# Two-block transformer layer, one core: the loop over further expert tiles stands ahead of the last step's products

## The chip, the core and the metric

The kernel runs on one core of one Trainium2 chip. The metric is device time in microseconds (us) of one execution. Engines are named as in the profile: PE (matrix products; PEld is its weight load), DVE, ACT, POOL and SP; SP only issues transfers and waits.

## What is computed

Two layers follow each other on 512 tokens of 1024 features in float32. The first has a gated short convolution, sparse attention and a dense feed-forward part. The second has latent attention, a convolution branch, and a mixture of 32 experts of which each token takes two; a last normalization ends it. All that this change touches lies in the mixture:

```python
a = jnp.einsum('td,edf->tef', t, e_gate[gi])
u = jnp.einsum('td,edf->tef', t, e_up[gi])
hid = jax.nn.silu(a) * u * combine[:, gi, :, None]
out = out + jnp.einsum('tef,efd->td', hid, e_down[gi])
...
x = x + gt2 * hierarchical_moe(...)
return rmsnorm(x, final_norm_g)
```

## The kernel before

The mixture works on tiles of tokens that were sorted by expert. Sixteen paired tiles hold up to 64 tokens of one expert and 48 of another. What does not fit goes into further tiles of 64 tokens of one expert. How many of these there are is known only at run time. The first further tile is always worked, as the last of 17 steps (step 16, group 16 in `seq`); the others are worked by `loop()` (L1679), a loop in hardware registers from 1 to a count read from the tile `ei` (L1683). In the profiled execution the count is 1, so the body is not run; what is run is the test of the loop and what stands at its exit.

A step i has these parts, each issued in program order (`keep`):

- `weights(i)` (L1640): the experts' weights come in thirds of 512 KB, each one transfer on SP's queue (L1293). A paired step takes six, step 16 takes three, by `further(0)` (L1629). Their buffers are a ring.
- `hidden(i)` (L1595): products of features and weights on PE (L1592), three of eight blocks first; then `turn(i - 1)` (L1702), which transposes the hidden rows of the step before on PE (L1609) and copies them out on DVE into `ht` (L1611); then the other five blocks; then the activation on ACT (L1603) and DVE (L1604) into `hs`.
- `rows_in_place(i + 1)` (L1697): transposed features of the next step's rows, in the tile `xtb`.
- `finish(i - 1)` (L1705): second products of the step before (`down`, L1620 on PE, L1621 on DVE into `y`). Up to step 14 an indirect transfer issued by POOL then adds the rows to the table `acc` in DRAM (L1625, "the add"). For steps 15 and 16 `keep_on_chip` (L1666) splits `y` into two parts (ACT L306, DVE L307) and makes a selection matrix `oh` (DVE L1670).

With LOOP = 16 the loop is issued at the end of step 16's turn in the Python loop: behind step 16's products and behind `finish(15)`, and in front of `turn(16)` and `finish(16)`. At the start of step 15 the program issues the weights of step 16 and after them the load of the last norm's gain (`gfin`: 512 KB into a row buffer, L1721). After the loop the table `acc` is loaded again in four transfers (`fin`, L1741, two on SP, two on ACT), PE adds the rows kept on chip by products with `oh` (L1751), and the last norm and the stores follow.

Before the loop's exit every engine waits, in a row of pair-wise semaphore waits, for every other engine and for every transfer queue: each engine's part of this is booked on L1684. The tiles `xwe`, `xtb` and the two `y` are in a pool of four buffers of 512 KB (`x_tile`, L466).

Of the kernel before, what the change touches and what calls it, by code (L numbers as in the profile page):

```python
# [72 lines left out]
GA1 = (0, 0, 0, 1, 0, 1, 0, 1, 1, 0)  # L73
NW = 9
NCH = 2
LOOP = 16
LF = True
NX = 18
NR = 8
# [157 lines left out]
def build(tc, A, out, taps=None):  # L237
# [35 lines left out]
    def psum(tag, name=None):  # L273
        return psp.tile([P, S], F32, tag=tag, bufs={"mm": 3, "lg": 2, "tp": 2, "po": 1}[tag],
                        name="p" + (name or tag))
# [167 lines left out]
    class Ssq:  # L443
# [4 lines left out]
        def add(self, t, scale=1.0, pin=False):  # L448
            sq = blk("sq" if self.acc else "acc")
            i = act(sq, t, ACT.Square, scale=scale)  # L450
            if pin:
                keep(i)
            if self.acc is None:
                self.acc = sq
            else:
                self.eng.tensor_tensor(self.acc, self.acc, sq, ALU.add)
# [9 lines left out]
    def x_tile(name):  # L466
        return xpool.tile([P, D], F32, tag="x", bufs=4, name=name)
# [14 lines left out]
    xg = []  # L482
# [412 lines left out]
    xg = []  # L895
    s1, s2 = Ssq(G), Ssq(G)
    r = None
    for half in range(2):
        hid = []
        st = {}  # L900
# [399 lines left out]
    def more(n, after=False):  # L1300
        for _ in range(n):
            e, j = THIRDS[len(we)]
            we[e, j] = load(A["we"][order[e]], j, after)
# [242 lines left out]
    def rows_of(ws):  # L1546
        return PR if len(ws) == 2 else 64
# [3 lines left out]
    def gather(xg, si_, n):  # L1551

        rows_in.append(keep(nc.gpsimd.indirect_dma_start(  # L1553
            out=xg[:n], out_offset=None, in_=htok,
            in_offset=bass.IndirectOffsetOnAxis(ap=si_[:n], axis=0), bounds_check=S - 1, oob_is_err=False)))
        return xg
# [4 lines left out]
    xtb = x_tile("xt")  # L1561
    yb = [x_tile("y%d" % i) for i in range(2)]
    ohb = ml[0].tile([P, S], F32R, name="oh")

    def scaled(n, xg, st):

        for q in range(2):
            o = slice(q * S, (q + 1) * S)
            keep(act(xg[:n, o], xg[:n, o], ACT.Copy, scale=st[:n, 2:3]))

    def features(n, xg, xt):

        xt = xt.rearrange("p (k t) -> p k t", k=DB)
        for q in range(2):
            pt = psum("tp")
            for j in range(4):
                k, o = 4 * q + j, slice(j * P, j * P + n)
                keep(nc.tensor.transpose(pt[:, o], xg[:n, k * P:(k + 1) * P], ident[:n, :n]))
            for j in range(4):
                k, o = 4 * q + j, slice(j * P, j * P + n)  # L1580
                if j % 2:
                    keep(act(xt[:, k, :n], pt[:, o], ACT.Identity, scale=gs2[:, k:k + 1],  # L1582
                             bias=adac[:, 24 + k:25 + k]))
                else:
                    keep(TS(xt[:, k, :n], pt[:, o], gs2[:, k:k + 1], adac[:, 24 + k:25 + k], ALU.mult, ALU.add))
        return xt

    def products(pg, ws, xt, ks):
        n = rows_of(ws)
        for k in ks:  # L1590
            for j, w in enumerate(ws):
                keep(mm(pg[64 * j:min(64 * j + 64, n), :256], xt[:, k, 64 * j:min(64 * j + 64, n)],  # L1592
                        w[k // 4][:, k % 4 * 256:(k % 4 + 1) * 256], start=(k == 0), stop=(k == DB - 1)))

    def hidden(ws, xt, st, between=None):  # L1595
        n = rows_of(ws)
        pg = psum("lg")
        products(pg, ws, xt, range(3))
        if between:
            between()  # L1600
        products(pg, ws, xt, range(3, DB))
        hs = mr[0].tile([P, 2, P], F32, tag="hs", bufs=2, name="hs")
        keep(act(hs[:n, 0], pg[:n, 0:128], ACT.Silu))  # L1603
        keep(STT(hs[:n, 1], pg[:n, 128:256], st[:n, 1:2], hs[:n, 0], ALU.mult, ALU.mult))  # L1604
        return hs

    def turned(n, hs):
        pt = psum("tp")
        keep(nc.tensor.transpose(pt[:, :n], hs[:n, 1], ident[:n, :n]))  # L1609
        ht = mr[0].tile([P, P], F32, tag="ht", bufs=2, name="ht")  # L1610
        keep(V.tensor_copy(ht[:, :n], pt[:, :n]))  # L1611
        return ht

    def down(ws, ht, y):
        n = rows_of(ws)
        for q in range(2):
            py = psum("mm")
            for j, w in enumerate(ws):
                o = slice(64 * j, min(64 * j + 64, n))
                keep(mm(py[o], ht[:, o], w[2][:, q * S:(q + 1) * S]))  # L1620
            keep(TT(y[:n, q * S:(q + 1) * S], py[:n], gt2r[:n, q * S:(q + 1) * S], ALU.mult))  # L1621
# [7 lines left out]
    def further(t):  # L1629

        ev = nc.sync.value_load(ei[0:1, bass.ds(t, 1)], min_val=0, max_val=31)
        src = A["we"][bass.ds(ev, 1)].rearrange("o p n -> p (o n)")
        return [[load(src, j) for j in range(3)]]
# [6 lines left out]
    def weights(i, after=True):  # L1640
        g = seq[i]
        if g == 16:
            wes[i] = further(0)
            return
        more(upto[g] - len(we), after)
        wes[i] = [[we[n, j] for j in range(3)] for n in (2 * g, 2 * g + 1)]
# [32 lines left out]
    def loop():  # L1679
        for j in range(LOOP + 1, 17):  # L1680
            weights(j, LF)

        ntl = nc.values_load(ei[0:1, 16:17], min_val=1, max_val=16)  # L1683
        with tc.For_i(1, ntl) as t:  # L1684
            st = mr[0].tile([P, 4], F32, name="lsl")[:, :3]

            nc.sync.dma_start(slots[16 * P:].rearrange("(g p) c -> p g c", p=P), slt[:, 16:])
            nc.sync.dma_start(st[:64], slots[bass.ds(16 * P + 64 * t, 64)])
            ix = mr[0].tile([P, 1], I32, name="lix")
            V.tensor_copy(ix[:64], st[:64, 0:1])  # L1690
            w = further(t)
            xg = gather(xgb[0], ix, 64)
            scaled(64, xg, st)
            down(w, turned(64, hidden(w, features(64, xg, xtb), st)), yb[0])
            add(64, yb[0], ix, acc)

    def rows_in_place(i):  # L1697
# [7 lines left out]
    def finish(i):  # L1705
        if i < 17 - NCH:
            down(wes.pop(i), hts.pop(i), yb[i % 2])
            add(size(i), yb[i % 2], sidx[:, seq[i]:seq[i] + 1], acc if seq[i] == 16 else halves[seq[i] // 8])
        else:
            keep_on_chip(i)  # L1710
# [4 lines left out]
    for i in range(17):  # L1715
        if i not in wes:
            weights(i)
        if i == 15:
            weights(16)
            gfr = xgb[i % NQ]  # L1720
            keep(nc.sync.dma_start(gfr, A["gfin"].broadcast_to([P, D])))  # L1721
        hss[i] = hidden(wes[i], xts.pop(i), slt[:, seq[i]], (lambda: turn(i - 1)) if i else None)
        if i < 16:
            rows_in_place(i + 1)
        if i < 15:
            scaled(size(i + 2), xgb[(i + 2) % NQ], slt[:, seq[i + 2]])
        if i:
            finish(i - 1)
        if i == LOOP:
            loop()  # L1730
    turn(16)
    finish(16)

    if LOOP == 17:
        loop()
# [70 lines left out]
```

## Time and profile before

| | us |
|---|---|
| median of three runs | 1369.53 (1366.01 to 1370.35) |
| the profiled execution | 1369.21 |
| its span, first to last instruction | 1367.4 |

The profile page gives busy times, the span in 40 slices, and the granted clock of PE in tenths of full speed. The timeline lists instructions of an engine in order: start and duration in us, line, operation, output and inputs, count, and in brackets the idle time ahead of it with what ended it. An entry "L1684" stands for the loop's test and exit on some engine. The list of windows gives each engine's busy time in a stretch, the granted clock, the busy share of the 16 transfer engines and the rate. PE's fp32 products count twice in the trace: one product in the program is two records.

### The profile page before, as it was taken

What the parts mean: (1) busy time and instruction counts of PE and PEld (TensorE: products, weight loads), DVE (VectorE), ACT (ScalarE), POOL (GpSimd) and SP (SyncE); (2) the same over time, 40 slices, a digit from 0 to 9 for tenths busy, and PEclk for the clock granted to TensorE, in tenths of its full rate; (3) what the DMA queues carried; (4) which work ended last, traced back from release to release, by engine and by line L of the source; (5) the groups of instructions that cost most, each with busy time, mean ns of one, the idle gap of its engine ahead of it and who ended that gap; (6) DMA issues with size and microseconds to landing.
All of it is one profiled execution on the core that took longest, in us unless ns stands there. A gap on an engine that the chain in (4) does not pass through costs nothing. (4 is left out here: it accounts for less than half of the span.)

```text
span 1367.4 us, 16340 instructions
## 1 busy us (share of the span) xinstructions
PE 1263.3 (92%) x5800; PEld 948.5 (69%) x5800; DVE 834.5 (61%) x1459; ACT 544.5 (40%) x898; POOL 643.8 (47%) x365
## 2 busy tenths in 40 slices
PE   6798999999999999999999988999979999689875
PEld 4576887777888878777788767778846587445432
DVE  5857785543758643367246577989977762644324
ACT  4433335666433332122324344243376542155322
POOL 4514447554646554444747645256734372123311
PEclk9999999999999999999999999899989999789997
DMA  5214323233245644565323223233330169989883
GB/s 166 71 51 152 103 91 139 87 107 123 93 138 186 203 164 142 190 246 197 112 85 103 71 93 93 73 120 132 116 108 24 48 245 367 339 290 277 264 298 124
DMA packets 69538, 206.02 MB, mean 151 GB/s; under 512 B 9539, under 2 KB 14331, under 8 KB 69456
## 3 DMA queue, kind: packets, MB, share of 16 engines
q1 hardware_dynamic: 60608, 190.67, 41.0%
q0 software_dynamic: 4048, 8.01, 2.5%
q10 hardware_dynamic: 4800, 6.29, 1.3%
q8 instruction: 46, 0.75, 0.2%
q14 instruction: 36, 0.29, 0.1%
HBM read 191.90 MB, written 21.61 MB: 156 GB/s over the span
## 5 line engine op out<-in xcount | busy, mean ns | idle before, releaser
L337 POOL TENSOR_TENSOR wl<-raw,wh 128x1024 fp32r<-128x1024 f32 (+2 forms) x180 | 420.2, 2337 | 440.4 <-ACT wh L336 336.1
L336 ACT ACTIVATE wh<-raw 128x1024 fp32r<-128x1024 f32 (+2 forms) x183 | 183.3, 1004 | 348.7 <-DMA raw<-in_w_dn 71.6
L345 PE MATMUL pw_gu<-xg,wh 128*128 128x512 f32 x704 | 168.6, 391 | 0.0
L345 PEld LDWEIGHTS pw_gu<-xg,wh 128*128 128x128 f32 x704 | 131.5, 188 | 31.3 <-issue 3.4
L701 DVE SCALAR_TENSOR_TENSOR ad<-raw,cact,ad 128x512 f32<-128x512 f32 x84 | 91.2, 1133 | 44.9 <-DMA raw<-in_ada 44.9
L345 PE MATMUL pw_cv<-h,wh 128*128 128x512 f32 x320 | 83.8, 416 | 8.9 <-ACT wh L336 6.2
L345 PE MATMUL pw_gu<-xg,wl 128*128 128x512 f32 x352 | 87.9, 390 | 0.0
L1039 DVE SCALAR_TENSOR_TENSOR ptaps<-u,vec,ptaps 128x511 f32<-128x511 f32 (+28 forms) x116 | 85.7, 739 | 3.3
L345 PE MATMUL pw_dn<-h,wh 128*128 128x512 f32 x352 | 85.5, 390 | 0.0
L1592 PE MATMUL plg<-we,xt 128*64 128x256 f32 (+1 forms) x528 | 74.4, 400 | 10.6 <-DMA we<-in_we 6.9
L345 PEld LDWEIGHTS pw_cv<-h,wh 128*128 128x128 f32 x320 | 63.9, 202 | 23.8 <-ACT wh L336 7.5
L345 PEld LDWEIGHTS pw_dn<-h,wh 128*128 128x128 f32 x352 | 65.9, 188 | 14.5 <-issue 0.8
L345 PEld LDWEIGHTS pw_gu<-xg,wl 128*128 128x128 f32 x352 | 65.8, 188 | 13.7
L1592 PEld LDWEIGHTS plg<-we,xt 128*64 128x64 f32 (+1 forms) x528 | 40.2, 135 | 42.0 <-issue 13.1
L345 PE MATMUL pw_gb<-h,wh 128*128 128x512 f32 x256 | 64.3, 394 | 0.0
L345 PE MATMUL pw_ga<-h,wh 128*128 128x512 f32 x256 | 62.3, 391 | 0.0
L345 PEld LDWEIGHTS pw_ga<-h,wh 128*128 128x128 f32 x256 | 47.7, 188 | 10.3 <-issue 0.8
L345 PEld LDWEIGHTS pw_gb<-h,wh 128*128 128x128 f32 x256 | 47.4, 188 | 9.2
L729 DVE TENSOR_SCALAR e<-e,ri 128x512 f32<-128x512 f32 (+2 forms) x64 | 48.2, 755 | 1.5
L1553 POOL DMA_INDIRECT xg<-htok,sidx x17 | 17.4, 1025 | 67.3 <-ACT xt L1582 43.9
L727 ACT ACTIVATE e<-e,mx 128x512 f32<-128x512 f32 (+2 forms) x64 | 40.8, 638 | 20.3 <-DVE mx L770 13.2
L907 POOL TENSOR_TENSOR t<-t,m 128x512 f32<-128x512 f32 x22 | 32.7, 1488 | 30.0 <-ACT t L906 30.0
(461 smaller groups left out, 2490.9 us busy)
## 6 DMA issues: line engine op xcount, KB each, us to landing
we<-in_we SPq DMA_DIRECT2D x99, 512.0 KB, 9.7
raw<-in_ada SPq DMA_DIRECT2D x48, 512.0 KB, 3.8
raw<-in_w_gu SPq DMA_DIRECT2D x44, 512.0 KB, 4.3
raw<-in_w_cv SPq DMA_DIRECT2D x20, 512.0 KB, 3.5
raw<-in_w_ga SPq DMA_DIRECT2D x16, 512.0 KB, 3.6
raw<-in_w_gb SPq DMA_DIRECT2D x16, 512.0 KB, 3.4
raw<-in_w_o SPq DMA_DIRECT2D x16, 512.0 KB, 3.5
spill<-g SPq DMA_DIRECT2D x24, 256.0 KB, 2.3
```

The lines of the kernel that those rows point to most:

```text
L336: act(wh[:, :n], raw[:, :n], ACT.Copy)
L337: (eng or G).tensor_tensor(wl[:, :n], raw[:, :n], f(wh[:, :n]), ALU.subtract)
L345: mm(ps, w[:, o + k * M:o + (k + 1) * M], xs[k][i], start=(first and j == 0), stop=(last and j == n - 1))
L701: STT(t, raw[:, o], cact[:, k:k + 1], t, ALU.mult, ALU.add)
L727: act(e, e, ACT.Exp, scale=-1.0, bias=mx[:, h_, b:b + 1], accum_out=sm[:, h_, b:b + 1])
L729: (G if b in NP else V).tensor_scalar(e, e, r, None, ALU.mult)
L907: G.tensor_tensor(t, t, r, ALU.mult)
L1039: keep(STT((a if k else y)[:, s:], u[:, :S - s], w, a[:, s:], ALU.mult, ALU.add))
L1553: rows_in.append(keep(nc.gpsimd.indirect_dma_start(out=xg[:n], out_offset=None, in_=htok, in_offset=bass.IndirectOffsetOnAxis(ap=si_[:n], ...
L1592: keep(mm(pg[64 * j:min(64 * j + 64, n), :256], xt[:, k, 64 * j:min(64 * j + 64, n)], w[k // 4][:, k % 4 * 256:(k % 4 + 1) * 256], start=( ...
```

## The change

LOOP is 15 in place of 16. So `loop()` is issued at the end of step 15's turn: behind `finish(14)`, and in front of step 16's products, `turn(15)`, `finish(15)`, `turn(16)` and `finish(16)`. The loop's body gets a feature tile of its own, `lxt`, since `xtb` now holds step 16's features while the loop stands. It is a fifth tile of the pool of four and takes the buffer of `xwe`. The line at the head of `loop()` that issues the weights of the steps from LOOP + 1 to 16 was empty before; it now issues `weights(16)` once more, after step 15 had already done so, and step 16 uses the second set.

```diff
-LOOP = 16
+LOOP = 15
...
     def loop():
         for j in range(LOOP + 1, 17):
             weights(j, LF)
+        lxt = x_tile("lxt")
 
         ntl = nc.values_load(ei[0:1, 16:17], min_val=1, max_val=16)
...
-            down(w, turned(64, hidden(w, features(64, xg, xtb), st)), yb[0])
+            down(w, turned(64, hidden(w, features(64, xg, lxt), st)), yb[0])
```

On PE before, from step 16's products to its second products (the rows between the two L1684 groups are the loop's body, which is not run; `plg` are hidden products, `ptp` transposed tiles, `pmm` second products):

```order
L1592 MATMUL plg<-we,xt 64x256 x3
L1609 MATMUL ptp<-cst,hs 128x112
L1592 MATMUL plg<-we,xt 64x256 x5
L1620 MATMUL pmm<-we,ht 64x512
...
L1684 COMPARE_AND_BRANCH
L1684 UNCONDITIONAL_BRANCH x2
...
L1609 MATMUL ptp<-cst,hs 128x64
L1620 MATMUL pmm<-we,ht 64x512 x2
```

On PE now, the same stretch:

```order
L1685 COMPARE_AND_BRANCH
L1685 UNCONDITIONAL_BRANCH x2
...
L1592 MATMUL plg<-we,xt 64x256 x3
L1609 MATMUL ptp<-cst,hs 128x112
L1592 MATMUL plg<-we,xt 64x256 x5
L1620 MATMUL pmm<-we,ht 64x512
...
L1609 MATMUL ptp<-cst,hs 128x64
L1620 MATMUL pmm<-we,ht 64x512 x2
```

The exit moved from between the second products of step 15 and the transposition of step 16 to ahead of step 16's first products.

On SP, as a piece of the difference, at the end of the weights (`gfin` is the gain):

```order
 L1293 DMA we<-in_we 128x1024
-L1721 DMA xg_9270<-in_gfin 128x1024
-L1684 COMPARE_AND_BRANCH
...
+L1293 ISA
+L1293 DMA we<-in_we 128x1024
+L1293 ISA
+L1293 DMA we<-in_we 128x1024
+L1293 ISA
+L1293 DMA we<-in_we 128x1024
+L1722 DMA xg_9270<-in_gfin 128x1024
+L1685 COMPARE_AND_BRANCH
```

Three more loads of 512 KB stand ahead of the gain's load and of the loop's test.

## Rows read from the trace of the kernel before

**Rows 1.** The page: span, and the granted clock of PE in 40 slices.
```profile
span 1367.4 us, 16340 instructions
PEclk9999999999999999999999999899989999789997
```
**Rows 2.** Timeline of PE, end of step 15 to the kept rows: start, duration, line.
```profile
1322.97 2.51 PE L1620 MATMUL pmm<-we,ht 128*64 128x512 f32 x8
1329.04 2.68 PE L1592 MATMUL plg<-we,xt 128*64 128x256 f32 x6 [3.56 <-SPq L1684]
...
1334.49 1.88 PE L1620 MATMUL pmm<-we,ht 128*64 128x512 f32 x7
1338.99 0.27 PE L1609 MATMUL ptp<-cst,hs 64*128 64x64 f32 x1 [2.63 <-DVEq L1684]
1340.49 3.67 PE L1620 MATMUL pmm<-we,ht 128*64 128x512 f32 x4 [1.22 <-DVE ht L1611]
1344.09 0.80 PE L1751 MATMUL ppo<-yh,oh 112*128 112x512 f32 x1
```
**Rows 3.** Waits of SP, 1310 to 1368 us: total, times, longest.
```profile
SPq L1684 <- DMA acc<-y,sidx: 5.5, 1, 5.5
SPq L1684 <- DVEq L1683: 2.7, 1, 2.7
```
**Rows 4.** The loop's lines by engine: duration ns min/median/max, first and last start.
```profile
L1683 POOLq TENSOR_LOAD <-ei x1: 496/496/496, 1326.6 to 1326.6; - x1
...
L1683 DVEq TENSOR_LOAD <-ei x1: 544/544/544, 1337.2 to 1337.2; - x1
...
L1684 PEldq EVENT_SEMAPHORE  x13: 51/51/364, 1336.4 to 1338.6; - x13
...
L1684 DVEq EVENT_SEMAPHORE  x13: 21/50/50, 1338.5 to 1339.9; - x13
```
**Rows 5.** Timeline of POOL, the last add; and L1625's times to landing, three adds.
```profile
1326.84 1.45 POOL L1625 DMA_INDIRECT acc<-y,sidx  x1 [8.02 <-DVE y L1621]
...
DMA to landing us min/median/max: 8.0/8.5/8.6
```
**Rows 6.** Windows: busy us per engine (PE, PEld, DVE, ACT, POOL), clock, transfer share, GB/s.
```profile
1300.00:1326.00 26.00, 21.59 (x128) 10.16 (x127) 8.78 (x23) 8.19 (x19) 3.90 (x3) 1.00 0.97 331
1328.00:1332.00 4.00, 2.96 (x7) 1.28 (x7) 0.00 (x0) 0.00 (x0) 0.29 (x1) 0.65 0.59 134
1332.00:1335.00 3.00, 3.00 (x16) 1.84 (x17) 0.28 (x2) 0.27 (x1) 0.00 (x0) 0.90 0.05 12
1341.00:1344.00 3.00, 3.00 (x4) 0.46 (x2) 0.85 (x3) 0.63 (x1) 0.00 (x0) 0.50 1.00 388
1339.40:1346.00 6.60, 5.51 (x9) 2.27 (x10) 2.94 (x6) 1.26 (x2) 0.00 (x0) 0.50 0.84 318
```
**Rows 7.** Timeline of SP: the last five weight loads, and the gain's.
```profile
1316.85 3.14 SPq L1293 DMA_DIRECT2D we<-in_we  x5
1320.52 0.34 SPq L1721 DMA_DIRECT2D xg<-in_gfin  x1
```
**Rows 8.** Timeline of DVE, between the second products of steps 15 and 16.
```profile
1335.59 1.52 DVE L1621 TENSOR_TENSOR y<-pmm,gt2r 112x512 f32<-112x512 f32 x2 [0.25 <-PE pmm L1620]
1337.03 0.68 DVE L307 TENSOR_TENSOR yl<-y,yh 112x512 fp32r<-112x512 f32 x1
1337.63 0.86 DVE L1670 TENSOR_SCALAR oh<-moeb,slt 64x128 fp32r<-64x128 bf16 x4
1340.21 0.22 DVE L1611 COPY ht<-ptp 128x64 f32<-128x64 f32 x1 [1.72 <-PE ptp L1609]
1340.35 0.68 DVE L307 TENSOR_TENSOR yl<-y,yh 112x512 fp32r<-112x512 f32 x1
```
**Rows 9.** Timeline of PE earlier: two runs of 14 products behind idle time.
```profile
1287.74 3.23 PE L1592 MATMUL plg<-we,xt 128*48 128x256 f32 x14 [2.57 <-DMA we<-in_we]
...
1299.87 1.93 PE L1592 MATMUL plg<-we,xt 128*48 128x256 f32 x14 [1.36 <-DMA we<-in_we]
```
**Rows 10.** Transfer queues, 1336 to 1340 us: packets, MB, share of 16 engines.
```profile
q8 instruction: 1, 0.02, 1.5%
```

## The prediction

> **What bounds the kernel now.** I read the page first [rows 1]: the granted clock is full nearly throughout, with dips at the very end, and the change touches only the last 45 us. There I read the timeline of PE [rows 2], since PE or what it waits for sets the end until the kept rows are added (L1751). The reader should see three things in it. First, PE ends step 14's second products at 1325.5 and stands idle for 3.56 us until step 16's first products at 1329.04. The row names SP's L1684, which in the program is no condition of that product; what it needs are its weights, so I read this wait as one for the transfers, which is borne out by the transfer share of 0.97 up to 1326 [rows 6]. Second, from the end of step 15's second products, 1334.49 + 1.88 = 1336.37, to step 16's second products at 1340.49 PE does only one transposition; the loop's exit lies in this gap of 4.12 us. Third, the second products of step 16 take 3.67 us for four records and run at a granted clock of 0.50, the lower level of 1.2 GHz; so does all from 1339.40 to 1346.00 [rows 6].
>
> Then the loop's own rows. POOL comes to the loop's test at 1326.6, DVE at 1337.2 [rows 4]. SP, in the exit, waits 5.5 us for the landing of the last add and then 2.7 us for DVE [rows 3]. The add is issued at 1326.84 and takes 8.0 us to land, 8.6 at most among the last three [rows 5], so it lands at 1334.8. Today this wait costs nothing, because PE and DVE work on steps 15 and 16 until 1336.4 and 1338.5; the exit is held by DVE, which comes last.
>
> **The change part by part.** The sum is made on the profiled execution, 1369.2 us (span 1367.4 and 1.8 around it); the median of the three runs is 1369.5, so nothing needs to be scaled.
>
> (a) *The exit now stands ahead of step 16's products.* Every engine must meet there, and every transfer must have landed. No engine has work left that it could do meanwhile: PE is done at 1325.5, DVE's last product of step 14 is out at about 1326.6, when POOL issues the add. So the exit opens when the last transfer lands, and the add alone puts that at 1334.8 (or 1335.4 with 8.6 us), 5.8 us after the time at which the products start today.
>
> (b) *Three more loads.* `weights(16)` is issued twice, and the second set stands on SP's queue ahead of the gain's load. Three loads of 512 KB are 1.573 MB. The queue is full at this place: share 0.97 at 331 GB/s from 1300 to 1326, and 388 GB/s is what a stretch without the adds gives [rows 6]. So they cost 4.05 to 4.75 us of transfer time. SP issues them behind the last five weight loads, in the place of the gain's load at 1320.52 [rows 7]; that many loads keep the transfer engines busy, so I count no gap between them. Where they end: the transfers' share falls from 0.59 (1328 to 1332) to 0.05 (1332 to 1335) [rows 6]. If the loads had run dry at 1332.0, the new end is 1336.1; if one transfer engine was busy with loads and add until 1334.8, it is 1339.6. These are the two ends. I take the middle, 1338.0: what is left behind 1332 is little, but the slowest engine decides when a load counts as landed. The gain's load is last of all; it isn't needed before the norm, but the exit waits for it too.
>
> (c) *The exit itself.* DVE's 13 waits run from 1338.5 to 1339.9, about 0.1 us each, when nothing holds them up any more; PE leaves its last one at 1338.6 and starts its next instruction at 1338.99 [rows 4, 2]. The wait for the add or the loads is among the first five of them in the listing of the program, so some eight remain: 0.8 us, and 0.4 to start, 1.2 in all. PE's first product comes at 1338.0 + 1.2 = 1339.2, against 1329.04: **+10.2 us** (with the add alone 1336.0, +7.0; at the far end 1340.8, +11.8).
>
> (d) *From the first product to step 15's last second product.* 1329.04 to 1336.37 today, 7.33 us, of which the first part is at the lower clock (0.65 from 1328 to 1332, 0.90 from 1332 to 1335) [rows 2, 6]. The same instructions follow the exit, behind a longer idle time, so they start at the lower clock too, and nothing else that they need is late. I take 0. If the clock comes back as late as it does after 1340.49, where it is still 0.50 at 1346.00 (5.5 us of work), instead of the some 3 us after 1329.04, about 2.4 us more run at half speed: +1.2.
>
> (e) *The gap of 4.12 us without the exit.* What remains in it is DVE's queue: the rows for `y` end at 1337.11, `yl` starts at 1337.03, `oh` at 1337.63 for 0.86, then the second `yl` (0.60 from start to start) and only then the copy to `ht`, 0.22 [rows 8]. In the changed order the second `yl` stands ahead of the copy (today behind it), so the copy starts at 1338.49 + 0.60 = 1339.09 and PE at about 1339.4, on today's scale, against 1340.49: **-1.1 us**. So most of the gap was never the exit's.
>
> (f) *The clock at step 16's second products.* PE idles for about 2.7 us there instead of 2.63 and 1.22. The nearest rows are those of steps 12 and 13: behind 2.57 us idle 14 records took 3.23 us, behind 1.36 us idle 1.93 [rows 9]. 2.7 is nearest to the first, so I take it that the clock falls as today: 0. If it does not, the 5.51 us of work at 0.50 between 1339.40 and 1346.00 [rows 6] take half: -2.8.
>
> (g) *Hidden.* The four loads of `fin` are issued right behind the exit, and so about 10 us ahead of their use relative to PE's work; they landed in time before. ACT issues two of them ahead of step 16's activation, 0.8 us beside PE's products of about 5 us. The tile `lxt` is used in the body alone, which is not run; it takes a buffer whose last readers are step 13's products. Nothing changes behind L1751.
>
> Sum: 10.2 - 1.1 = +9.1, and 1369.2 + 9.1 = **1378.3 us**. Ends: 7.0 - 1.1 - 2.8 = +3.1 (1372.3) and 11.8 - 1.1 + 1.2 = +11.9 (1381.1).
>
> A rule that would add to this: in these 4 us there is one transfer of the instruction queue [rows 10], 1.5% of 16 engines, so about 1 us on one engine; PE nevertheless starts 0.4 us after its last wait [rows 2, 4]. The Trainium skill, "Runtime: NRT & Kernel Launch", section "Instruction fetch mechanics", says that a taken branch whose target lies outside of the window already fetched stalls until the page has come. The trace before shows no such stall at this exit; by the rule the sum would be about 1379 to 1380, where the fetch falls behind the exit.
>
> **The rivals.**
> *The add alone (R1).* The three loads end before the add lands or with it, as the thin share behind 1332 allows. Then the first product comes at 1336.0: 7.0 - 1.1 = +5.9, 1375.1 us. For it: the share of 0.05. Against it: all transfer engines are shared, and 4 us of loads behind 1332 end at 1336 at the earliest.
> *A meeting that hides (R2), not slower.* PE is idle for 3.56 us at this place anyway. If the exit opens by the time at which the weights come, it costs nothing, the gap of (e) shrinks and the clock may hold: from 1369.2 - 1.1 = 1368.1 down to 1365.3 with (f). It decides at a first product at 1330.1 or before (1.1 after today's). Between that and 1334.3 the result is within 0.3%. Against it: SP's wait of 5.5 us for the add [rows 3] shows that the exit does wait for transfers; for it, only that the add might be issued or land earlier, of which no row shows a sign.
> *A late fetch or a late clock (R3).* The instructions behind the exit, or the clock as in (d), come later than today: 1.2 us for either, both 2.4: 1379.5 to 1380.7 us. One row speaks for the clock (1340.49 to 1346), one against it (1329.04 on); for the fetch none [rows 10]. The page named above is the rule for it.
> *The change doesn't do what it says.* The order of instructions shows that the loop and the loads did move, so this gets nothing.
>
> **How the numbers follow.** Forecast 0.60; R1 0.20; R2 0.10 (of which 0.03 faster); R3 0.10. About 0.3%, 4.1 us, is what a measurement of this kernel can tell from no change: 1365.1 to 1373.3. R1 with a clock that holds would end at 1372.3, so 0.02 of it goes to "within". Faster 0.03, same 0.09, slower 0.88. The range takes in the forecast's ends and R1 and leaves out R2: 1373.0 to 1381.0.
>
> **What would show it.** Right: PE's idle time ahead of step 16's first product grows from 3.56 to about 13.7 us and is booked on L1685; SP's longest wait there is for a weight load or the gain, landing around 1338, with the add before it; 1.2 us from landing to product; about 7.3 us to the end of step 15's second products; then 3.0 us, not 4.1, to step 16's; the rest as long as before. Wrong: a first product at 1336 (R1), one before 1331 (R2), or a gap behind step 15's second products that stays at 4 us. The forecast falls altogether if the exit does not wait for the add, or if the second set of loads is landed before the add is issued.

## The result, and the profile after

The changed kernel takes 1379.64 us (median of 5 executions, 1376.98 to 1382.23) against 1369.53 (5 executions, 1366.01 to 1370.68). The ratio is 1.0073, with a 95% interval of 1.0051 to 1.0095: it is slower, by 10 us (7.0 to 13.0 by the interval). The forecast was 1378.3, the range 1373.0 to 1381.0. The profiled execution of the changed kernel took 1377.4 us, with a span of 1375.6.

The timeline of PE over the place (the same columns as in [rows 2]: start, duration, line, operation, count, and in brackets the idle time ahead and what ended it):

```profile
1324.67 1.92 PE L1620 MATMUL pmm<-we,ht 128*48 128x512 f32 x6 [0.32 <-DMA we<-in_we]
1340.24 2.82 PE L1592 MATMUL plg<-we,xt 128*64 128x256 f32 x6 [13.65 <-issue]
...
1345.45 1.88 PE L1620 MATMUL pmm<-we,ht 128*64 128x512 f32 x7
1347.26 0.27 PE L1609 MATMUL ptp<-cst,hs 64*128 64x64 f32 x1
1350.24 3.40 PE L1620 MATMUL pmm<-we,ht 128*64 128x512 f32 x4 [2.71 <-DVE ht L1611]
1353.57 0.50 PE L1752 MATMUL ppo<-yh,oh 112*128 112x512 f32 x1
```

PE ends step 14's second products at 1326.59 and then stands idle for 13.65 us, where it stood for 3.56 before [rows 2]. In return, from the end of step 15's second products (1345.45 + 1.88 = 1347.33) to those of step 16 (1350.24) it is 2.91 us in place of 4.12.

What the long wait is for, the chain of waits says (the pieces that led to the last instruction, in order of time: start, us, what):

```profile
1326.93 12.20 DMA xg<-in_gfin
1339.13 1.11 issue
1340.24 2.82 PE plg L1592 x6
```

The product does not read the gain (`gfin`). It stands behind the exit, and the exit waited for the gain's landing. SP's waits in the exit (1310 to 1376 us; total, times, longest) have all three kinds of transfer in them. The list is sorted by total and not by time; the order is that of the landings in the trace: the add at 1336.0, the last load of the second set at 1337.9, the gain at 1339.1.

```profile
SPq L1685 <- DMA we<-in_we: 1.9, 1, 1.9
...
SPq L1685 <- DMA acc<-y,sidx: 1.5, 1, 1.5
SPq L1685 <- DMA xg<-in_gfin: 1.2, 1, 1.2
```

So the last load of the second set was waited for 1.9 us behind the add, and the gain 1.2 us behind that. Before, SP waited 5.5 us for the add here, and then for DVE [rows 3]; DVE is not waited for any more.

The windows show what was in flight (stretch, us; busy us of PE, PEld, DVE, ACT, POOL; granted clock, transfer share, GB/s):

```profile
1326.00:1329.00 3.00, 0.59 (x2) 0.00 (x0) 1.15 (x2) 0.12 (x1) 1.40 (x1) 1.00 1.02 416
1329.00:1332.00 3.00, 0.00 (x0) 0.00 (x0) 0.00 (x0) 0.00 (x0) 0.05 (x1) 0.56 1.04 400
1332.00:1335.00 3.00, 0.00 (x0) 0.00 (x0) 0.00 (x0) 0.00 (x0) 0.00 (x0) 0.50 0.62 157
1335.00:1338.00 3.00, 0.00 (x0) 0.00 (x0) 0.00 (x0) 0.00 (x0) 0.00 (x0) 0.50 0.19 71
1338.00:1341.00 3.00, 0.76 (x2) 0.52 (x3) 0.00 (x0) 0.00 (x0) 0.00 (x0) 0.50 0.03 11
```

The transfers run at their full rate up to 1332 and then thin out for 7 us: 157, 71, 11 GB/s. No engine does any work to speak of from 1329 to 1339. So most of the exit's wait is not for a full queue. The trace tells what it is for: each load raises its semaphore sixteen times as its parts land, and of the gain's sixteen parts twelve had landed by 1334.5 and the last four between 1336.3 and 1339.1. A load counts as landed with its last part. The granted clock falls in the idle stretch from 1.00 to 0.50, the lower of its two levels (1.2 GHz).

A measure that is useful below is the **path**: from the end of step 14's second products to the first placed row (`ppo<-yh,oh`, L1751 or a line near it). All that the change moves lies in it. Before it is 1344.09 - 1325.48 = 18.61 us, after 1353.57 - 1326.59 = 26.98: +8.37 us. Of that +10.09 is the idle time, -0.24 the way to the end of step 15's second products (7.09 us in place of 7.33), -1.21 the gap, and -0.27 step 16's second products (3.40 in place of 3.67). Ahead of the path this execution was 1.1 us later, and behind it 1.3 us shorter, which has to be held against what two executions of one kernel differ by.

### The profile page after: what moved, and what is told of

It reads as the page before. It is cut to its first block, busy times and chain, and to the rows that moved or that the text cites. A ratio compares the mean times of both kernels' runs of the same rounds, so it can differ in the third digit from the quotient of the medians.

```text
span 1375.6 us, 16347 instructions
## 1 busy us (share of the span) xinstructions
PE 1265.6 (92%) x5800; PEld 950.7 (69%) x5800; DVE 838.2 (61%) x1459; ACT 544.7 (40%) x898; POOL 645.0 (47%) x365
## 4 chain that ended last, share of the span: by engine, by line
PE 69%; DVE 13%; DMA 9%; issue 4%; ACT 3%; POOL 1%; SPq 0%; DVEq 0%; ACTq 0%; POOLq 0%
PE pw_gu L345 16%; PE pw_dn L345 7%; PE pw_cv L345 6%; PE pw_gb L345 5%; DMA we<-in_we 4%; PE pw_o L345 4%; PE plg L1592 3%; DVE ptaps L1039 3%; PE pw_ga L345 3%; PE pmm L1620 2%; PE pw_co L345 2%; PE pw_ya L345 2%; PE ppo L1135 2%; DMA raw<-in_w_cv 1%; PE pw_qk L345 1%
## 5 line engine op out<-in xcount | busy, mean ns | idle before, releaser
L1592 PE MATMUL plg<-we,xt 128*64 128x256 f32 (+1 forms) x528 | 73.3, 396 | 20.5 <-issue 13.6
L345 PEld LDWEIGHTS pw_cv<-h,wh 128*128 128x128 f32 x320 | 65.9, 208 | 24.3 <-ACT wh L336 7.6
L345 PEld LDWEIGHTS pw_gu<-xg,wl 128*128 128x128 f32 x352 | 65.8, 188 | 13.7
```

The source lines that it names most:

```text
L345: mm(ps, w[:, o + k * M:o + (k + 1) * M], xs[k][i], start=(first and j == 0), stop=(last and j == n - 1))
```

## The experiments

The theory: the exit in its new place costs the wait for the last transfer that is in flight, whatever it is, and about 1.1 us from its landing to the product (written "issue" in the chains). The rivals are, in different runs, that the exit costs a fixed time there, that only the add matters, and that the difference is an offset of a kernel as it is loaded and nothing of its code.

| kernel | idle ahead of step 16, us | path, us | ratio to before, 95% interval |
|---|---|---|---|
| before | 3.56 | 18.6 | - |
| before, unchanged, as a kernel of its own (`e0_before_again`) | 3.26 | 18.1 | 1.0024 [1.0007, 1.0040] |
| after | 13.65 | 27.0 | 1.0073 [1.0051, 1.0095] |
| after, measured again (`e6_after_again`) | 13.11 | 27.0 | 1.0069 [1.0043, 1.0095] |
| after, one weight set (`e1_one_set`) | 10.01 | 23.9 | 1.0039 [1.0014, 1.0064] |
| after, no add (`e3_no_add`) | 11.59 | 25.5 | one execution, 1375.35 us |
| after, one set, no add (`e3b_one_set_no_add`) | 7.53 | 21.4 | 1.0011 [0.9994, 1.0028] |
| the same, gain behind the exit (`e8_nothing_in_flight`) | 6.08 | 19.6 | 1.0000 [0.9982, 1.0018] |
| after, gain behind the exit (`e9_gain_behind`) | 13.19 | 27.1 | 1.0050 [1.0034, 1.0067] |
| before, two weight sets (`e2_two_sets`) | 9.36 | 24.3 | 1.0033 [1.0017, 1.0048] |
| before, no loop (`e4_no_loop`) | 2.93 | 16.6 | 0.9993 [0.9971, 1.0015] |
| before, loop behind step 16's products (`e5_loop_mid`) | 3.26 | 21.5 | 1.0004 [0.9984, 1.0024] |
| before, loop there and step 16 turned early (`v2_turn_early`) | 1.83 | 13.6 | 1.0031 [1.0016, 1.0047] |
| the same again (`e7_v2_again`) | 3.00 | 15.5 | 1.0019 [0.9993, 1.0045] |

The path is worked out from PE's timeline of each kernel's profiled execution, as above.

### How much two equal kernels differ

The kernel before, unchanged, was measured as if it were a changed one; and the changed kernel was measured again.

> The kernel before, unchanged, once more. It tells how far two measurements of one kernel lie apart, and gives a second trace. In the traces so far step 0's first product of the mixture starts anywhere from 1202 to 1209 us, before anything that the change touches. Theory (that spread is of the execution and not of the kernel): ratio within 0.997 to 1.003 of the kernel before, the stretch from step 0's first product to the end 165 us as in its first trace, within 2 us. Rival (each kernel as loaded has a fixed offset of its own ahead of the mixture): the ratio itself lies off 1 by 0.2 to 0.4%.

> The changed kernel, unchanged, on the chip of the other experiments. Theory (the loss is in the stretch from step 0's first product to the end, which was 171.7 us in its first trace against 165.0): ratio 1.005 to 1.009, the stretch 170 to 174 us. Rival (a part of the measured loss was an offset ahead of the mixture): ratio 1.002 to 1.004.

The unchanged kernel came out 0.24% slower than itself, with an interval that leaves out 1. By this one pair, a ratio of up to about 0.25% says nothing here about code, however narrow its interval; whether it is an offset of the kernel as loaded or of this one comparison isn't shown. The changed kernel came out at +0.73% and +0.69%, which such an offset doesn't make. The +0.69% and the unchanged kernel's +0.24% were taken against the same executions of the kernel before: against the unchanged kernel's own 1373.13 us the changed one's 1378.49 is 0.39% more, still above what the pair differs by. Its path in the trace is the same to 0.02 us, which is luck in part: 0.54 us less idle time and 0.54 less in step 16's second products, and 1.09 more on the way between. PE in the second execution of the kernel before, then in that of the changed one:

```profile
1336.15 2.02 PE L1592 MATMUL plg<-we,xt 128*64 128x256 f32 x6 [3.26 <-SPq L1684]
...
1350.93 0.50 PE L1751 MATMUL ppo<-yh,oh 112*128 112x512 f32 x1
```

```profile
1338.60 2.82 PE L1592 MATMUL plg<-we,xt 128*64 128x256 f32 x6 [13.11 <-issue]
...
1349.69 2.86 PE L1620 MATMUL pmm<-we,ht 128*64 128x512 f32 x4 [2.70 <-DVE ht L1611]
1352.48 0.80 PE L1752 MATMUL ppo<-yh,oh 112*128 112x512 f32 x1
```

In the unchanged kernel step 16's products started 7 us later than in [rows 2], with the same path (18.1 us). What moved this execution by 7 us lies ahead of step 16, and is no matter of the change: the first product of the mixture already started 8.0 us later (1210.42 against 1202.40). The path (+8.4 and +8.9 us) is the sharper figure for what the change costs.

### One set of weights, or no add, or neither

```diff
     def loop():
-        for j in range(LOOP + 1, 17):
+        for j in range(LOOP + 2, 17):
             weights(j, LF)
```

> The changed kernel without the second set of step 16's weights: the loop stays ahead of step 16's products, but only three loads and the gain's load stand in front of it. Theory (the exit opens when the last transfer lands, and the second set is 3 to 4 us of that): the exit opens when the last add lands, about 1335 to 1336; first product of step 16 near 1336.5 in place of 1340.2, and the time falls by 3 to 4.5 us against the changed kernel, to about 1375.5; still 4 to 6.5 us above the kernel before. Rival (the exit and its branch cost this by themselves, the loads end under the add): the first product stays near 1340 and the time near 1379.5. Rival (the second set is the whole loss, the loop's place costs nothing): 1369 to 1370.

```diff
-            add(size(i), yb[i % 2], sidx[:, seq[i]:seq[i] + 1], ...)
+            if i != 14:
+                add(size(i), yb[i % 2], sidx[:, seq[i]:seq[i] + 1], ...)
```

> The changed kernel without the add of step 14's rows (the last transfer that POOL issues ahead of the exit is left out, and with it a part of the result). In the changed kernel's trace the add landed at 1336.0, the last weights at 1337.9, the gain at 1339.1, and the transfer share was low from 1332 on. Theory A (the add's packets hold up a few transfer engines, and the loads behind them): without it the loads land 1.3 us apart to the end and the exit opens 2 to 3 us earlier against the last second products of step 14: the idle time ahead of step 16's first product is 10.5 to 12 us in place of 13.65. Theory B (the loads land late by themselves): 13 to 14 us as before.

> The changed kernel without the second weight set and without the add of step 14's rows (that part of the result is left out). Idle time of TensorE before step 16's first product: 13.65 us with both, 10.0 without the set alone, 11.6 without the add alone. Theory A (the exit opens when the last transfer in flight has landed): the last transfer left is the gain, issued about 2 us before the last products of step 14 end; idle 4 to 7 us, first product 7 to 9 us earlier than in the changed kernel, time 1369 to 1374 (kernel before +0 to +0.3%). Rival (the exit itself, in its new place, costs most of the idle time whatever is in flight): idle 8.5 us or more, time 1374 to 1377.

The chains of waits of the three (the changed kernel without the second set, without the add, without both):

```profile
1330.77 7.68 DMA acc<-y,sidx
1338.45 1.33 issue
1339.78 2.82 PE plg L1592 x6
```

```profile
1326.24 10.07 DMA xg<-in_gfin
1336.31 1.11 issue
1337.42 2.82 PE plg L1592 x6
```

```profile
1318.11 12.20 DMA xg<-in_gfin
1330.32 0.59 issue
1330.90 2.82 PE plg L1592 x6
```

In each the piece ahead of step 16's products is a transfer that these products don't need: the add where the second set is gone, the gain where the add is gone. The four idle times (both 13.65 and 13.11, add alone 10.01, set alone 11.59, neither 7.53) can be read in pairs: the set costs 4.06 us without the add and 3.1 to 3.6 with it; the add costs 2.48 us without the set and 1.5 to 2.1 with it. So the set weighs more than the add, and the add still costs time where it is not the last to land. The landings show how: the last five loads of the changed kernel landed at 1331.97, 1334.06, 1336.60, 1337.87 and 1339.13, without the add at 1331.23, 1332.51, 1333.78, 1335.05 and 1336.31. Undisturbed they land 1.3 us apart, and the add, in flight at the same time, holds them up by 2.1 us in all. Neither rival holds alone.

In `e1_one_set` the first product came at 1339.78, where 1336.5 was expected and "near 1340" was the rival's sign; but step 14 ended 3.2 us later in that execution, so it is the idle time that decides, and it fell as the theory has it. The miss is in the last: with neither, 4 to 7 us were expected and 7.53 came, because the gain's load still took 12.20 us from issue to landing, as long as with everything else in flight.

The time agrees with the order of the paths: one set less takes the ratio from 1.0073 and 1.0069 to 1.0039, about 4 us, though the intervals overlap; without both it is 1.0011, within what an unchanged kernel shows.

### The gain behind the exit

The gain's load was still in front of the exit in all of these. In two kernels it is issued behind the second of SP's loads of `fin`.

```diff
-            gfr = xgb[i % NQ]
-            keep(nc.sync.dma_start(gfr, A["gfin"].broadcast_to([P, D])))
...
-        (nc.scalar if FQ and b % 2 else nc.sync).dma_start(fin[b], ...)
+        ld = (nc.scalar if FQ and b % 2 else nc.sync).dma_start(fin[b], ...)
+        if b == 2:
+            gfr = xgb[15 % NQ]
+            with tc.issue_after(ld.ins):
+                nc.sync.dma_start(gfr, A["gfin"].broadcast_to([P, D]))
```

> The changed kernel without the second weight set, without the add of step 14's rows (that part of the result is left out), and with the gain's load issued behind the exit, so that only step 16's own weights are in flight ahead of the exit. Theory A (the exit costs the wait for the last transfer in flight, and about 1.1 us from there): with the gain's load in front TensorE stood idle for 7.53 us; now the weights land last, which the kernel before waits for anyway within 3.3 to 3.6 us, so the idle time is 4.4 to 6.0 us and the first row of the placed products comes 18.3 to 19.9 us behind step 14's products (18.1 and 18.6 in the kernel before). Rival (a fixed cost of the exit in its new place, whatever is in flight): idle time 7 us or more.

> The changed kernel with the gain's load alone issued behind the exit; the second set and the add stay in front of it. Theory A: the gain's landing was the last, 1.2 us behind the second set's; without it the exit opens with the second set: idle time of TensorE 11.0 to 12.6 us against 13.65 and 13.11, path from step 14's products to the first placed row 24.5 to 26.4 us against 27.0, time 1 to 2.5 us under the changed kernel's. Rival (the add or the shared transfer engines set the end, the gain is only an onlooker): idle time 13 us or more.

Their chains, first with nothing but step 16's own weights in flight, then the changed kernel with only the gain moved:

```profile
1322.97 11.77 DMA we<-in_we
1334.74 0.70 issue
1335.43 2.82 PE plg L1592 x6
```

```profile
1327.62 13.72 DMA we<-in_we
1341.34 1.31 issue
1342.66 2.82 PE plg L1592 x6
```

With only step 16's weights in flight the exit costs 6.08 us of idle time, 2.5 to 2.8 more than the kernel before, and the path is 1.0 to 1.5 us longer; the ratio is 1.0000. That is just above what the theory expected (4.4 to 6.0), the path is within it (18.3 to 19.9), and it speaks against a fixed cost of 7 us or more: taking the load away took 1.45 us. The 2.5 us that are left are the exit's demand for all thirds of the weights, while the first products want only those that they read: the first third landed at 1332.21 and the last at 1334.74, and 0.70 us from there is the exit's own.

The second kernel is a miss. Without the gain 11.0 to 12.6 us were expected; 13.19 came, and the path is 27.1 as with it. The chain names the last weight load, which landed 11.9 us behind the end of step 14's products (1341.34 against 1329.47), where the gain had landed 12.5 us behind it in the changed kernel and 11.9 in its repetition. By the idle time alone the gain would be the last to land, but not the cause. The landings say otherwise. What differs is where the end of step 14's products falls in the row of loads: step 15's last weight load landed 2.14 us behind it here, and 1.55 and 0.87 us in the two executions with the gain. Counted from that load (1328.14, 1326.36 and here 1331.60), the last transfer landed 10.99 and 11.03 us later with the gain and 9.74 without it. So taking the gain away did save 1.3 us, and the later row of loads ate it up. The same count gives 8.91 us without the add, 5.10 with neither set nor add, and 3.81 with the gain behind the exit too: so the add holds up the end by 2.1 us (10.99 to 8.91), the second set by 3.8 (8.91 to 5.10) and the gain by 1.3 (5.10 to 3.81, and 10.99 to 9.74). The ratio of 1.0050 can't be told from 1.0069 by its interval.

### The second set without the moved exit

The kernel before, with `weights(16)` issued once more at step 15 and the second set used.

> The kernel before (loop behind step 15's second products) with the second set of weights added at the same place of SP's queue. On DVE the scheduler now puts yl and oh behind the loop's exit. Theory (transfers are the bound at this place): step 16's products wait for the second set, whose first third landed near 1334.1 in the changed kernel's trace against 1328.9 in the one before, so the first product comes some 5 us later, and since DVE meets the exit earlier in its own queue the sum is +3.5 to +5.5 us against the kernel before: 1373 to 1375. Rival (only the place of the exit matters): 1369 to 1370, the second set hidden by the work of steps 15 and 16.

```profile
1335.66 2.79 PE L1592 MATMUL plg<-we,xt 128*64 128x256 f32 x6 [9.36 <-SPq L1684]
```

The idle time grows from 3.56 to 9.36 us with the exit where it was, since step 16's products read the later set. So the loads alone bring 5.7 us of path (24.3), and the exit alone, in `e1_one_set`, 5.3 (23.9). Together they bring 8.4 and not 11, since they are waited for at the same time. The time went up by 0.33%, which is 4.5 us, of which an offset as in the unchanged kernel may be a part. The kernel isn't the change's other half in every row: DVE's rows for `yl` and `oh` stand behind the exit in it.

### The kernel before without the loop

> The kernel before without the loop over further tiles (its body is not run with these inputs; the test and the exit go). Theory (of the 4.1 us between the second products of steps 15 and 16 only 1.1 are the exit's, the rest is DVE's queue): gap of 3.0 us, -1.1 us, or up to -3.5 if the clock then holds: 1366 to 1368.5. Rival (the exit is the whole gap): gap near 1 us, -3 to -6 us: 1363.5 to 1366.

```profile
1341.08 0.27 PE L1609 MATMUL ptp<-cst,hs 64*128 64x64 f32 x1
1344.06 3.50 PE L1620 MATMUL pmm<-we,ht 128*64 128x512 f32 x4 [2.71 <-DVE ht L1611]
```

With no loop at all, the gap between the second products of steps 15 and 16 is 1344.06 - 1341.15 = 2.91 us: the same as in the changed kernel. So of the gap of 4.12 us before, 1.2 us was the exit's and 2.9 DVE's. The path is 1.4 to 2.0 us shorter than before; with the rest of the order as it is, this is all that any place for the exit could win there, and the time (0.9993) doesn't show it.

### Other places for the exit

The loop right behind step 16's products (`hidden(16)`), and the same with step 16's transposition moved in front of step 15's last work:

```diff
+        if i == LOOP:
+            loop()
         if i < 16:
             rows_in_place(i + 1)
...
-        if i == LOOP:
-            loop()
```

```diff
         down(wes.pop(i), hts.pop(i), y)
+        if i == 15:
+            turn(16)
...
-    turn(16)
```

(In the second, the rows `yl` and `oh` are also ordered behind the copy to `ht`.)

> The kernel before with the loop alone moved from behind finish(15) to right behind hidden(16): the whole of step 15's second half stands behind the exit, and the second set of weights is not loaded twice. Theory A: the exit still waits for the last transfer in front of it, step 14's add; it was ready before the exit already, so the first product after the wait is not later; the gap between step 15's two groups of second products (4.1 us with the exit in it) falls to 2.7 to 3.0 us, and the exit shows up behind the first products of step 16 at up to 2 us of TensorE. Time -2.5 to +1.5 us against the kernel before, ratio 0.998 to 1.001 before the offset of a kernel as loaded (0.24% seen for an unchanged one). Rival (any place of the exit between the steps costs what the changed kernel showed): ratio 1.005 or more.

> The kernel before with two changes: the loop stands right behind step 16's hidden products (ahead of step 15's second products), and step 16's transposition and its copy on DVE stand directly behind step 15's second products, ahead of yl and oh. Theory (the exit is cheap where the last add has just landed, near 1335; what holds PE in the gap is DVE's yl and oh ahead of the copy): the exit costs about 1.4 us between the products and step 15's second products, the gap shrinks from 4.1 to about 1 us, net -1.7 us, and the clock stays full for another -2.8: 1365 (1364 to 1368). Rival (the exit is dear at any place where PE has work behind it): step 15's second products start 3 us later or more and the time is 1369.5 or above.

> The kernel with the loop right behind step 16's hidden products and the early transposition, once more: its first trace was 159.9 us from step 0's first product to the end, 5.1 us shorter than that of the kernel before, but its median was 0.3% above. Theory (the stretch is really shorter, the first median carried an offset ahead of the mixture): ratio 0.994 to 1.000, stretch 159 to 162 us. Rival (other executions have a longer exit than the profiled one): ratio 1.002 to 1.005 again, and a second trace with a stretch of 164 us or more.

PE with the loop moved alone, then with the early transposition, then the latter's second measurement:

```profile
1335.74 3.57 PE L1620 MATMUL pmm<-we,ht 128*64 128x512 f32 x8 [2.14 <-DVEq L1684]
1339.25 0.28 PE L1609 MATMUL ptp<-cst,hs 64*128 64x64 f32 x1
1342.70 3.62 PE L1620 MATMUL pmm<-we,ht 128*64 128x512 f32 x4 [3.17 <-DVE ht L1611]
1346.24 0.50 PE L1751 MATMUL ppo<-yh,oh 112*128 112x512 f32 x1
```

```profile
1340.93 1.93 PE L1622 MATMUL pmm<-we,ht 128*64 128x512 f32 x8 [3.04 <-issue]
...
1343.79 1.93 PE L1622 MATMUL pmm<-we,ht 128*64 128x512 f32 x4 [0.73 <-DVE ht L1613]
1345.65 0.50 PE L1760 MATMUL ppo<-yh,oh 112*128 112x512 f32 x1
```

```profile
1338.87 1.93 PE L1622 MATMUL pmm<-we,ht 128*64 128x512 f32 x8 [2.13 <-DVEq L1694]
...
1350.04 0.63 PE L1760 MATMUL pmm<-yl,oh 112*128 112x512 f32 x1
```

Moved alone, the exit makes PE wait 2.14 us behind step 16's products, and the gap behind step 15's second products did not shrink (3.39 us from 1339.31 to 1342.70, and its 3.17 us of wait for DVE are above the 2.7 to 3.0 expected). The path is 3 us longer, in part because all second products ran at half speed; the time (1.0004) doesn't show that either. With the early transposition the path is the shortest of all, 13.6 and 15.5 us, because both groups of second products run at full speed and the gap is 1 us. Yet the time is 0.31% and 0.19% above the kernel before: 1364 to 1368 us had been expected, and 1375.13 came. In the second execution the placed rows gave it back: they ran at half clock (0.63 us a row in place of 0.40), and from the first of them to the end of the span it took 28.0 us in place of 22 to 23. The stretch from the mixture's first product to the end took 165.6 us, which was the rival's sign (164 or more). In the first execution they did not (23.6 us), and the stretch took 159.9 against 165.0 before; there the mixture had started 7.0 us later. So a shorter path didn't make a faster kernel here, and why not is open: two profiled executions don't show it, and an offset as large as that of the unchanged kernel would hide it. A hint is that the single executions line up by their mean granted clock (in the second measurement 1365.35 us at 0.968 and 1379.65 at 0.954), so others may have lost time as the second profiled one did; this isn't shown. No kernel among these beats the one before.

## Why the prediction was right

Taken by its own steps, on the path: forecast +9.1 us, measured +8.4 (and +8.9 by the repetitions).

(a) *The exit opens when the last transfer lands.* Shown: the chains of the changed kernel and of its variants name that transfer, and which one it is changes with what is in flight. No engine had work in the meantime, as the windows show.

(b) *The three loads: last landing at 1338.0.* The term was right in sum, but two errors lie in it that cancel by luck. Step 14 ended 1.1 us later in this execution, so relative to that the forecast was 12.5 us and the set landed at 11.3; and the gain behind it, for whose own landing I had counted nothing, came 1.2 us later. The three loads, put at 4.05 to 4.75 us, cost 3.81 by the landings (8.91 against 5.10 us without the add), and beside them the add held the loads up. How I came to the end was the weaker part, a middle between two guesses on when the loads run dry. In the kernel before the last weights had landed at 1331.4 and the gain, which that guess left out, only at 1334.2. So the question was when the last part of the last load lands, as the prediction said of the slowest engine, and not the rate.

(c) *1.2 us from landing to product.* Measured 1.11 and 1.21 in the two executions of the changed kernel, 0.59 to 1.33 in the others. The idle time came out as 13.65 us, against 13.7 as forecast; that it is this close is the luck of (b), and the repetition has 13.11.

(d) *The way to step 15's last second product, 0 (+1.2).* It was 7.09 us in place of 7.33, and in the repetition 8.18 (1338.60 to 1344.90 + 1.88), where the clock came back later. Both lie within the ends.

(e) *The gap, -1.1.* Measured -1.21 (2.91 in place of 4.12). The chain of the changed kernel shows DVE's queue filling it, row after row:

```profile
1347.38 0.69 DVE y L1621
1348.08 0.60 DVE yl L307
1348.67 0.78 DVE oh L1670 x4
1349.45 0.60 DVE yl L307
1350.05 0.15 DVE ht L1611
```

The kernel without the loop has the same 2.91 us, so this is settled by a run.

(f) *The clock at step 16's second products, 0.* They took 3.40 us and 2.86 in place of 3.67; the clock fell as before, in the repetition only while they ran (0.77 from 1350 to 1351, then 0.50). It came back earlier in the first execution, where the placed rows start at 0.50 us, against 0.80 [rows 2]. From the first of them to the end of the span it takes 22.0 us, against 23.3 before. But the unchanged kernel's second execution took 22.4, so this isn't to be put down to the change.

(g) *Hidden.* Nothing of it shows.

**The rivals.** R1, that the add alone decides, fell: the gain and the set land later. The kernel that makes it true, with one set, has 10.01 us of idle time and a ratio of 1.0039, about the 1375.1 us that R1 gave. R2 fell with the idle time. R3 gave 1379.5 to 1380.7, and the median of 1379.64 would fit it, but by the wrong cause: a late fetch would stand between landing and product. These rows are PE's waits and branches in the exit (duration ns min/median/max, first and last start):

```profile
L1685 PEldq EVENT_SEMAPHORE  x13: 51/51/51, 1326.6 to 1339.9; - x13
...
L1685 PEldq COMPARE_BRANCH  x3: 101/179/304, 1325.4 to 1340.0; - x3
```

PE's last branch starts at 1340.0 and its product at 1340.24. The rule on taken branches that the prediction took from the Trainium skill, "Runtime: NRT & Kernel Launch", section "Instruction fetch mechanics", did not show as a price at this exit: there is no room for a stall. Whether the branch's target lay outside of the window already fetched, which is that rule's condition, no run shows. That the median is 1.3 us above the forecast is within what an unchanged kernel differs by.

## What to carry to other kernels

The exit of a run-time loop is a meeting of all engines and all transfers, even where the body isn't run. Put it where engines have work of their own while the last transfers land, and ask of each transfer issued ahead of it whether it could be issued behind. A second load of data that is already on chip isn't free because a wait stands there anyway: it moves the wait. Before calling a transfer an onlooker, look at the landings of all of them: idle time in single executions also moves with where the work ends in the row of loads. Measure an unchanged kernel as a changed one before believing a few tenths of a per cent.

## What was not expected of the hardware

*The tail of the loads.* Where the chain names the last load (six executions), it took 10.1 to 13.7 us from issue to landing, and 12.20 us both with the second set and the add in flight and without either. In the changed kernel, behind the stretch at 400 GB/s, come some 7 us in which 157, 71 and 11 GB/s are moved. The landings fit this: most parts of each load have landed by then and a few have not; the last parts of successive loads still land 1.3 us apart, which for 512 KB is about the full rate. One load less shortens this by 1.3 us, the add's absence by 2.1. Why some parts lag is open.

*The clock behind like idle times.* Step 15's eight second products took 3.57 us behind 2.14 us of idle time in one kernel and 1.93 us behind 2.13 us in another, both with some 3 us of idle time and 5 to 6 us of products before that. The idle time right ahead of a group doesn't tell which level it gets; terms that hang on the clock, as in (d) and (f), need both ends.

*Offsets of equal kernels.* Two profiled executions of the same code reached step 16's products at 1329.04 and 1336.15 us, and a measurement of the unchanged kernel against itself gave 1.0024 [1.0007, 1.0040].
